# Hybrid decoder layer with a product-key expert feed-forward: gate value products on ScalarE, gate copies beside their own step, six weight buffers instead of three, new paces for the gathered rows

## The chip, the cores and the metric

The kernel runs on one core of one Trainium2 chip. The metric is the device time of one execution in microseconds (us); the time given is the median of three runs. Five engines work side by side, each on its own queue in order: PE (TensorE), DVE (VectorE), ACT (ScalarE), POOL (GpSimd) and SP (SyncE, which here issues the weight loads).

## The reference, cut to what matters

One layer: three gated token mixers on 256 tokens of width 1024, then a product-key expert layer, which takes two thirds of the time and is where the change lies. For every token and each of 8 heads, 16 of 16384 experts are chosen with softmax weights g, and then

```
a = gelu(einsum('btd,bthkd->bthk', hi, u_tab[expert]))
w = g * a
return einsum('bthk,bthkd->btd', w, v_tab[expert])
```

The tables `u_tab` and `v_tab` hold 16384 rows of 1024 float32 each, 64 MB per table.

## The kernel before, in words

The 256 tokens are split. For 160 of them (ND) the kernel computes all experts densely: the whole u table is streamed, 128 jobs of 128 experts (`u_job`, L1098), each 8 float32 products with 160 tokens into one of two PSUM tiles `pj`; Gelu on ACT moves the result into one slot of `RA` (jobs 0 to 63) or `RC` (64 to 127). Then the v table is streamed in 128 jobs (`v_job`, L1122), which sum over the slots. Between the two, the slots must be multiplied by the gate, a matrix that is zero except where a token chose an expert. The gate is built in 40 gate steps of 4 tokens: DVE makes one-hot rows `oo` (L1136) and multiplies two of them by the gate values, kept as two float16 parts, into `gi` (L1138); PE makes the gate of the 4 tokens in a PSUM tile `pg` with 8 small products (`g_mm`, L1143); `g_apply` (L1154) puts it down: ACT copies it to slots that no job has filled yet (L1163), which the later job then multiplies (L1108, L1111, L1112), and DVE multiplies it into filled slots (L1166).

For the other 96 tokens (NS) the chosen rows are gathered by index: 96 gathers of 128 rows from the u table, each followed by a dot product on DVE (L1044), then 96 from the v table, each followed by a weighted sum on DVE (L1049). One such row step (`x_step`, L1039) takes a row tile out of a ring of 6 (half a megabyte each), and then has POOL issue the gather for the tile six steps on (`x_load`, L1029, the indirect DMA of L1036).

The order of all queues is written by the program. After u job i, `run_todo` (L880) adds a pace to a purse and issues row steps at a cost of 1.2 each: pace 0.35 before the gates are open, 1.0 after, 1.45 in the v stage (`X_PACE`, L41). The selection of the experts is finished during the u stage; then `open_gates` (L1216) frees its memory and gate steps start, spread over the remaining jobs by `rate` (L1248). Both weight streams use one pool of three 1 MB tiles (`RAW_BUFS`, L42, pool `rawp`, L55), one for two jobs; `load_raw` (L65) issues the load on SP's queue, `ahead_split` (L259) says how far ahead (L271).

Of the kernel before, what the change touches and what calls it, by code (L numbers as in the profile page):

```python
# [10 lines left out]
F32 = mybir.dt.float32  # L11
F32R = mybir.dt.float32r
BF = mybir.dt.bfloat16
F16 = mybir.dt.float16
I32 = mybir.dt.int32
U32 = mybir.dt.uint32
AF = mybir.ActivationFunctionType
OP = mybir.AluOpType
# [12 lines left out]
GT = 4  # L31
N_G = ND // GT
# [5 lines left out]
N_X = 2 * NS  # L38
N_WARM = 12
SEL_PACE = 1.85  # L40
X_PACE = (0.35, 1.0, 1.45)  # L41
RAW_BUFS = 3  # L42
S_BUFS = 3
X_BUFS = 2 * S_BUFS
# [3 lines left out]
def hybrid_block(ctx, tc, xt, memt, wst, cmpw, subk, cols, cpe, fng, ut, vt, un, out):  # L48
    nc = tc.nc
# [5 lines left out]
    rawp = ctx.enter_context(tc.tile_pool(name="rawp", bufs=RAW_BUFS))  # L55
# [2 lines left out]
    psj = ctx.enter_context(tc.tile_pool(name="psj", bufs=2, space=PSUM))  # L58
    ctx.enter_context(tc.manual_schedule())

    raws = {}

    nc.scalar.preload_act_table_set("natural_log_exp_and_others")

    def load_raw(r):  # L65
        kind, i = raw_list[r]
        t = rawp.tile([128, 2, 1024], F32, name="raw")
        src = {"w": wst, "u": ut, "v": vt}[kind]
        nc.sync.dma_start(t, src[2 * i:2 * i + 2].rearrange("n p c -> p n c"))
        raws[r] = t  # L70


    raw_list = [("w", i) for i in range(N_W // 2)]
    job_raw = {}
# [16 lines left out]
    next_raw = [0]  # L91

    def prefetch(n):
        while next_raw[0] < min(n, len(raw_list)):
            load_raw(next_raw[0])
            next_raw[0] += 1
# [140 lines left out]
    order = [("w", i) for i in range(N_W)] + list(u_order)  # L237
# [16 lines left out]
    def ahead(key):  # L254
        run_deferred(pre=True)
        ahead_split(key)
        run_deferred()

    def ahead_split(key):  # L259
        n = pos[key] + LOOK  # L260
        while done_split[0] <= min(n, len(order) - 1):
            k = order[done_split[0]]
            r = job_raw[k[0], k[1] // 2]
            prefetch(r + 1)
            if k[0] == "w":
                split(k, 2 if k == ("w", 1) else 1)
            done_split[0] += 1
            nxt = done_split[0]
            if nxt < len(order):
                prefetch(job_raw[order[nxt][0], order[nxt][1] // 2] + 1)  # L270
        prefetch(min(len(raw_list), job_raw[order[min(n, len(order) - 1)][0], order[min(n, len(order) - 1)][1] // 2] + RAW_BUFS - 1))  # L271

    hA1 = big.tile([128, 8, T], F32R, name="hA1")
    hA2 = big.tile([128, 8, T], F32R, name="hA2")
# [488 lines left out]
    for j in range(8):  # L763
# [4 lines left out]
        a = s1[key].rearrange("p (k c) -> p k c", k=8)  # L768
# [41 lines left out]
    for ks in (range(0, 6), range(6, 8)):  # L810
        for i in range(2):
            a = s1["w", 58 + i].rearrange("p (k c) -> p k c", k=8)
# [37 lines left out]
    ring = ctx.enter_context(tc.tile_pool(name="ring", bufs=1))  # L850
# [3 lines left out]
    RA = ring.tile([128, 64, ND], F32, name="RA")  # L854
# [4 lines left out]
    sel = se.enter_context(tc.tile_pool(name="sel", bufs=1, side="right"))  # L859
# [20 lines left out]
    def run_todo(names, purse, budget):  # L880
        debt[purse] += budget
        while True:
            n = next((n for n in names if todo[n]), None)
            if n is None:
                debt[purse] = 0.0
                return
            if todo[n][0][0] > debt[purse]:
                return
            c, f = todo[n].pop(0)
            debt[purse] -= c  # L890
            f()

    def tick2(budget):
        run_todo((1, 0), "s", budget)
# [13 lines left out]

    io16 = sel.tile([128, 16], F16, name="io16")
    nc.gpsimd.iota(io16, pattern=[[1, 16]], base=0, channel_multiplier=0, allow_small_or_imprecise_dtypes=True)  # L910
    gt = ring.tile([128, N_G, 4, GT], F16, name="gt")
    sd, sel_done = {}, []

    def sel_open(t):
# [65 lines left out]
    def sel_e(t):  # L980
        p = psg.tile([128, 3, 128], F32, name="pg")
        for n, src in enumerate((sd["r", t, 0], sd["r", t, 1], sd["bv", t])):
            nc.tensor.transpose(p[:, n], src.rearrange("p h k -> p (h k)"), ident)
        nq_ = min(32, N_G - t * 32)
        g = gt[:, t * 32:t * 32 + nq_].rearrange("p q n e -> p n q e")
        pe = p[:, :, 0:nq_ * GT].rearrange("p n (q e) -> p n q e", e=GT)
        nc.scalar.activation(g[:, 0:3], pe, AF.Copy)
        nc.vector.tensor_tensor(g[:, 3], pe[:, 2], g[:, 2], op=OP.subtract)
        sel_done.append(t)


# [2 lines left out]
    xa = ring.tile([128, NS], F32, name="xa")  # L994
    xw = ring.tile([128, NS], F32, name="xw")
    xcol = [sum(m for _, m, _ in X_GROUPS[:g]) for g in range(len(X_GROUPS))]
    xrow, x_free, x_next = {}, [0], [0]

    def x_move(dst, src, g, c, n):
# [29 lines left out]
    def x_load(n):  # L1029
        if n >= N_X:  # L1030
            return
        g, c = X_ORDER[n % NS]
        c += xcol[g]
        t = (sp1, sp2)[n % 2].tile([128, D], F32, name=("s1", "s2")[n % 2])
        src = un if n < NS else vt.rearrange("a b c -> (a b) c")
        nc.gpsimd.indirect_dma_start(t, None, src, bass.IndirectOffsetOnAxis(ap=xi[:, c:c + 1], axis=0))  # L1036
        xrow[n] = t

    def x_step(n):  # L1039
        t = xrow.pop(n)  # L1040
# [50 lines left out]
    slots = {}  # L1091
# [22 lines left out]
    gs = {}  # L1114
# [7 lines left out]
    def v_job(i):  # L1122
        ahead(("v", i))
        for c in range(8):
            v_mm(i, c)
# [4 lines left out]
    def g_prep(q):  # L1130
        if q >= N_G:
            return
        oo = gp.tile([128, 4, 128, 2], F16, name="oo", tag="g2", bufs=4)
        gi = gp.tile([128, 2, 2, 128, 2], F16, name="gi", tag="g2", bufs=4)
        tk = gt[:, q].rearrange("p n (a e) -> p (n a) e", e=2)
        nc.vector.tensor_tensor(oo, io2[:, None].to_broadcast([128, 4, 128, 2]),  # L1136
                                tk[:, 0:4, None, :].to_broadcast([128, 4, 128, 2]), op=OP.is_equal)
        nc.vector.tensor_tensor(gi, oo[:, None, 0:2].to_broadcast([128, 2, 2, 128, 2]),  # L1138
                                tk[:, 4:8].rearrange("p (s a) e -> p s a e", s=2)[:, :, :, None, :]
                                .to_broadcast([128, 2, 2, 128, 2]), op=OP.mult)  # L1140
        gs[q] = (oo, gi)

    def g_mm(q):  # L1143
        if q >= N_G:
            return
        oo, gi = gs.pop(q)
        p = psg.tile([128, GT, 128], F32, name="pg")
        for k in range(GT):
            for s in range(2):
                nc.tensor.matmul(p[:, k], oo[:, 2 + k // 2, :, k % 2], gi[:, s, k // 2, :, k % 2],  # L1150
                                 start=(s == 0), stop=(s == 1))
        gs["p", q] = p

    def g_apply(q, n):  # L1154

        if ("p", q) not in gs:
            return
        c = slice(q * GT, q * GT + GT)
        pv = gs.pop(("p", q)).rearrange("p t i -> p i t")
        for dst, i0 in ((RA, 0), (slots["RC"], 64)):  # L1160
            m = min(max(n - i0, 0), 64)
            if m < 64:
                nc.scalar.activation(dst[:, m:, c], pv[:, i0 + m:i0 + 64], AF.Copy, scale=1.0 / GSCALE)  # L1163
            if m:
                d = dst[:, 0:m, c]
                nc.vector.scalar_tensor_tensor(d, pv[:, i0:i0 + m], 1.0 / GSCALE, d, op0=OP.mult, op1=OP.mult)  # L1166
        g_done[0] = q + 1
# [48 lines left out]
    def open_gates():  # L1216
        nonlocal gp
        se.close()
        hb.close()
        gp = ctx.enter_context(tc.tile_pool(name="gp", bufs=2))  # L1220
        rc = ctx.enter_context(tc.tile_pool(name="rc", bufs=1))
        slots["RC"] = rc.tile([128, 64, ND], F32, name="RC")
        g_prep(0)

    gp, q, opened, rate, owed = None, 0, False, 0.0, 0.0
    for i in range(128):
        owed += rate
        step_g = owed >= 1.0
        if step_g:
            owed -= 1.0  # L1230
            g_prep(q + 1)
            g_apply(q - 1, i)
        u_job(i)
        if step_g:
            g_mm(q)
            q += 1
        if i == 0:
            scores(14)
            scores(15)
            select(1)  # L1240
            select(0)
            x_rows()
        if not opened:
            tick2(SEL_PACE if i < 90 else 1e9)
            opened = len(sel_done) == 2
            if opened:
                open_gates()
                rate = (N_G + 2) / (125.0 - i)  # L1248
        run_todo(("x",), "x", X_PACE[0] if not opened else X_PACE[1])
    fg = big.tile([128, D], F32, name="hA1")  # L1250
    nc.gpsimd.dma_start(fg, bass.AP(tensor=fng.tensor, offset=fng.offset, ap=[[0, 128], [1, D]]))
# [2 lines left out]
    for g, (o, m, r) in enumerate(X_GROUPS):  # L1254
        for s in range(r):
            nc.vector.tensor_tensor(fold[:, g, o:o + m], fold[:, g, o:o + m], ident[:, s * m:s * m + m], op=OP.add)
    for i in range(125):
        v_job(i)
        run_todo(("x",), "x", X_PACE[2] if i < 118 else 1e9)
    for i in range(125, 128):  # L1260
        ahead(("v", i))

# [127 lines left out]
```

## Time and profile before

| what | us |
|---|---|
| median of 3 runs (lowest, highest) | 976.77 (976.39, 977.38) |
| the profiled execution's own time | 975.81 |
| its span in the trace | 974.1 |
| busy: PE, DVE | 912.5 (94%), 659.3 (68%) |
| busy: POOL, ACT | 321.1 (33%), 240.8 (25%) |
| moved by DMA | 285.12 MB, mean 293 GB/s |

The profile is of one execution and 1.7 us shorter than that execution's time. In it the u jobs run from 308 to 629 us, the gate steps from 452 to 624 us, and the v jobs from 630 to 960 us. A float32 job of 8 products stands as 16 PE instructions. Busy PE is not PE at its peak, since matmuls overlap: the start of one group to the start of the next is what a job takes. A wait is put down to what ended last.

### The profile page before, as it was taken

The numbers are of one execution on the slowest core, as the hardware profiler recorded it, in microseconds if no ns is written. First come the engines' busy times: TensorE is split into PE (matmuls) and PEld (weight loads), VectorE is DVE, ScalarE is ACT, GpSimd is POOL, SyncE is SP. The second block draws the span as 40 slices with busy tenths as digits, with TensorE's granted clock in tenths as the row PEclk, the third lists the DMA queues.
The fourth block names the chain that finished last, engine by engine and source line by source line (L and its number), as shares of the span: only waits on it lengthen the run. The fifth ranks groups of instructions, "written<-read, shape, count | busy, mean of one in ns | idle before, by whom it ended". The sixth has DMA issues, their size and how long they took to land.

```text
span 974.1 us, 17019 instructions
## 1 busy us (share of the span) xinstructions
PE 912.5 (94%) x6807; PEld 868.2 (89%) x6807; DVE 659.3 (68%) x1410; ACT 240.8 (25%) x585; POOL 321.1 (33%) x346
## 2 busy tenths in 40 slices
PE   8999999998998999999999999998999989999894
PEld 6999999898998999999999989988888888888884
DVE  7757677657678788998888899844444444544442
ACT  4754688744433112112111111100000000000001
POOL 7702000036740143113343344343333333333301
PEclk8999999999999999999999999999999999999998
DMA  7734444335543698888999999999999999999971
GB/s 281 240 130 141 155 139 140 137 126 171 174 145 115 197 391 295 312 309 313 377 371 353 364 351 359 370 408 408 408 410 408 408 409 408 409 409 408 408 306 43
DMA packets 76318, 285.12 MB, mean 293 GB/s; under 512 B 6880, under 2 KB 6928, under 8 KB 75856
## 3 DMA queue, kind: packets, MB, share of 16 engines
q1 hardware_dynamic: 47152, 181.15, 50.7%
q0 software_dynamic: 28800, 102.61, 26.9%
q8 instruction: 53, 0.87, 0.4%
q10 hardware_dynamic: 288, 0.29, 0.1%
q14 instruction: 25, 0.20, 0.1%
HBM read 282.63 MB, written 1.05 MB: 291 GB/s over the span
## 4 chain that ended last, share of the span: by engine, by line
PE 46%; DMA 24%; DVE 22%; ACT 3%; POOL 2%; issue 2%; POOLq 0%; SPq 0%; ACTq 0%
DMA raw<-in_vt_dram 23%; PE po L1119 11%; PE pj L1104 8%; PE pj L232 6%; DVE s L1044 6%; PE pj L233 6%; PE pj L234 6%; DVE gi L1138 2%; DVE oo L1136 2%; DVE RA L1166 1%; ACT RC L1163 1%; POOL t L782 1%; DMA raw<-in_ut_dram 1%; DVE RC L1112 1%; PE z L233 1%
## 5 line engine op out<-in xcount | busy, mean ns | idle before, releaser
L1104 PE MATMUL pj<-hA,raw 128*128 128x160 f32 x2048 | 291.2, 301 | 7.8 <-ACT ga L1111 5.8
L1104 PEld LDWEIGHTS pj<-hA,raw 128*128 128x128 f32 x2048 | 279.9, 190 | 11.2 <-ACT ga L1111 8.0
L1049 DVE SCALAR_TENSOR_TENSOR acc<-s,xw,acc 128x1024 f32<-128x1024 f32 x94 | 120.8, 1285 | 126.7 <-DMA s<-in_vt_dram,xi 126.7
L1036 POOL DMA_INDIRECT s<-in_un_dram,xi x96 | 113.0, 1177 | 210.8 <-DVE xa L1044 120.0
L1119 PE MATMUL po<-RC,raw 128*128 128x160 f32 x1024 | 148.8, 302 | 14.1 <-DMA raw<-in_vt_dram 13.3
L1119 PE MATMUL po<-RA,raw 128*128 128x160 f32 x1024 | 147.6, 302 | 15.0 <-DMA raw<-in_vt_dram 15.0
L1119 PEld LDWEIGHTS po<-RA,raw 128*128 128x128 f32 x1024 | 139.9, 190 | 22.7 <-DMA raw<-in_vt_dram 21.7
L1119 PEld LDWEIGHTS po<-RC,raw 128*128 128x128 f32 x1024 | 140.2, 190 | 22.4 <-DMA raw<-in_vt_dram 20.3
L1036 POOL DMA_INDIRECT s<-in_vt_dram,xi x96 | 90.4, 942 | 161.6 <-DVE acc L1049 147.5
L1044 DVE CUSTOM_DVE_ANT_0 s<-s,hA 128x1024 f32<-128x1024 f32 x96 | 116.8, 1219 | 37.6 <-DMA s<-in_un_dram,xi 37.5
L202 DVE TENSOR_TENSOR s<-raw,s 128x1024 fp32r<-128x1024 f32 (+1 forms) x77 | 100.7, 1312 | 28.7 <-ACT s L201 28.4
L201 ACT ACTIVATE s<-raw 128x1024 fp32r<-128x1024 f32 (+1 forms) x84 | 86.5, 1035 | 68.8 <-PE pj L233 45.0
L232 PE MATMUL pj<-hA,s 128*128 128x256 f32 x336 | 99.0, 295 | 0.1
L234 PE MATMUL pj<-hA,s 128*128 128x256 f32 x336 | 95.0, 283 | 0.0
L233 PE MATMUL pj<-hA,s 128*128 128x256 f32 x336 | 95.0, 283 | 0.0
L232 PEld LDWEIGHTS pj<-hA,s 128*128 128x128 f32 x336 | 64.3, 191 | 3.3 <-issue 1.8
L1181 ACT ACTIVATE RA<-pg 128x512 f32<-128x512 f32 x2 | 1.2, 592 | 263.1 <-PE pg L1272 263.1
L233 PEld LDWEIGHTS pj<-hA,s 128*128 128x128 f32 x336 | 64.3, 191 | 0.6 <-issue 0.5
L234 PEld LDWEIGHTS pj<-hA,s 128*128 128x128 f32 x336 | 64.2, 191 | 0.0
L1108 ACT ACTIVATE RA<-pj 128x160 f32<-128x160 f32 x64 | 19.3, 304 | 120.8 <-PE pj L1104 120.8
L1163 ACT ACTIVATE RC<-pg 128x256 f32<-128x256 f32 (+39 forms) x40 | 11.4, 284 | 123.1 <-DVE RA L1166 123.1
L780 POOL TENSOR_TENSOR t<-t,t 128x256 f32<-128x256 f32 x7 | 5.1, 734 | 106.0 <-DVE t L779 106.0
(340 smaller groups left out, 1257.9 us busy)
## 6 DMA issues: line engine op xcount, KB each, us to landing
raw<-in_ut_dram SPq DMA_DIRECT2D x64, 1024.0 KB, 7.6
raw<-in_vt_dram SPq DMA_DIRECT2D x64, 1024.0 KB, 10.5
raw<-in_wst_dram SPq DMA_DIRECT2D x39, 1024.0 KB, 5.0
raw<-in_wst_dram SPq DMA_DIRECT2D x4, 512.0 KB, 7.5
s<-in_un_dram,xi POOLq DMA_INDIRECT x96, 8.2
s<-in_vt_dram,xi POOLq DMA_INDIRECT x96, 14.2
x<-in_memt_dram SPq DMA_DIRECT2D x1, 1024.0 KB, 7.1
cw<-in_cmpw_dram POOLq DMA_DIRECT2D x1, 1024.0 KB, 7.3
```

Source lines behind the costliest of these rows:

```text
L201: nc.scalar.activation(a[:, c], src[:, c], AF.Copy)
L202: eng.tensor_tensor(b[:, c], src[:, c], a[:, c].bitcast(F32), op=OP.subtract)
L232: nc.tensor.matmul(dst, l1, r1, start=first, stop=False)
L233: nc.tensor.matmul(dst, l1, r2, start=False, stop=False)
L234: nc.tensor.matmul(dst, l2, r1, start=False, stop=last)
L1036: nc.gpsimd.indirect_dma_start(t, None, src, bass.IndirectOffsetOnAxis(ap=xi[:, c:c + 1], axis=0))
L1044: nc.vector.tensor_tensor_reduce(t, t, hnat[:, g], 1.0, 0.0, OP.mult, OP.add, xa[:, c:c + 1])
L1049: nc.vector.scalar_tensor_tensor(acc[:, g], t, xw[:, c:c + 1], acc[:, g], op0=OP.mult, op1=OP.add)
L1104: nc.tensor.matmul(p, a[:, k], hT[:, k, 0:ND], start=(k == 0), stop=(k == 7))
L1119: nc.tensor.matmul(po[c // 2][:, c % 2], a[:, c * 128:c * 128 + 128], slot(i), start=(i == 0 and c % 2 == 0), stop=(i == 127), skip_group_ ...
L1136: nc.vector.tensor_tensor(oo, io2[:, None].to_broadcast([128, 4, 128, 2]), tk[:, 0:4, None, :].to_broadcast([128, 4, 128, 2]), op=OP.is_equal)
L1163: nc.scalar.activation(dst[:, m:, c], pv[:, i0 + m:i0 + 64], AF.Copy, scale=1.0 / GSCALE)
```

## The change

The gate values are kept in float32 (`gv`: the value, and what float16 loses of it). The product of one-hot rows and gate values moves from one DVE instruction (1024 elements) to eight ACT instructions of 128 elements each with a scale per partition (`g_gi`). `g_apply` is cut in two: the copies on ACT (`g_copy`) are issued right after the gate product of their own step, the DVE products at the start of the next job. From `open_gates` on a second pool of three weight tiles takes turns with the first, and loads are issued up to five tiles ahead instead of two. Row steps have pace 1.3 instead of 1.0 in the gate stage, and in the v stage the steps that are left are spread evenly over 116 jobs.

```diff
-X_PACE = (0.35, 1.0, 1.45)
+X_PACE = (0.35, 1.3)
...
-    raws = {}
+    raws, more = {}, {"from": None, "depth": RAW_BUFS - 1}
...
-        t = rawp.tile([128, 2, 1024], F32, name="raw")
+        pool = rawp if more["from"] is None or (r - more["from"]) // RAW_BUFS % 2 else more["pool"]
+        t = pool.tile([128, 2, 1024], F32, name="raw")
...
-        prefetch(min(len(raw_list), job_raw[...] + RAW_BUFS - 1))
+        prefetch(min(len(raw_list), job_raw[...] + more["depth"]))
...
-    gt = ring.tile([128, N_G, 4, GT], F16, name="gt")
+    gt = ring.tile([128, N_G, 2, GT], F16, name="gt")
+    gv = ring.tile([128, N_G, 2, GT], F32, name="gv")
...
-        nc.scalar.activation(g[:, 0:3], pe, AF.Copy)
-        nc.vector.tensor_tensor(g[:, 3], pe[:, 2], g[:, 2], op=OP.subtract)
+        hi = sel.tile([128, 32, GT], F16, name="hi")[:, 0:nq_]
+        nc.scalar.activation(g, pe[:, 0:2], AF.Copy)
+        nc.scalar.activation(v[:, :, 0], pe[:, 2], AF.Copy)
+        nc.scalar.activation(hi, pe[:, 2], AF.Copy)
+        nc.vector.tensor_tensor(v[:, :, 1], pe[:, 2], hi, op=OP.subtract)
...
-        nc.vector.tensor_tensor(gi, oo[:, None, 0:2].to_broadcast([128, 2, 2, 128, 2]),
-                                tk[:, 4:8].rearrange("p (s a) e -> p s a e", s=2)[:, :, :, None, :]
-                                .to_broadcast([128, 2, 2, 128, 2]), op=OP.mult)
-        gs[q] = (oo, gi)
+        gs["o", q] = oo
+
+    def g_gi(q):
+        if q >= N_G:
+            return
+        oo = gs.pop(("o", q))
+        gi = gp.tile([128, 2, 2, 128, 2], F16, name="gi", tag="g2", bufs=4)
+        for s in range(2):
+            for k in range(GT):
+                nc.scalar.activation(gi[:, s, k // 2, :, k % 2], oo[:, k // 2, :, k % 2], AF.Copy,
+                                     scale=gv[:, q, s, k:k + 1])
+        gs[q] = (oo, gi)
...
+        more["pool"] = ctx.enter_context(tc.tile_pool(name="raw2", bufs=RAW_BUFS))
+        more["from"], more["depth"] = next_raw[0], 2 * RAW_BUFS - 1
...
     for i in range(128):
+        if late is not None:
+            g_apply(late, i)
+            late = None
         owed += rate
-        step_g = owed >= 1.0
+        step_g = owed >= 1.0 and q < N_G
         if step_g:
             owed -= 1.0
             g_prep(q + 1)
-            g_apply(q - 1, i)
         u_job(i)
         if step_g:
             g_mm(q)
+            g_copy(q, i + 1)
+            g_gi(q + 1)
+            late = q
             q += 1
...
-                rate = (N_G + 2) / (125.0 - i)
+                g_gi(0)
+                rate = N_G / (124.0 - i)
...
+    x_done = [k for k in range(N_X) if k not in xrow and k < x_seen[0]]
+    pace = 1.2 * (N_X - len(x_done)) / 116.0
     for i in range(125):
         v_job(i)
-        run_todo(("x",), "x", X_PACE[2] if i < 118 else 1e9)
+        run_todo(("x",), "x", pace if i < 118 else 1e9)
```

## Rows read from the trace of the kernel before

**Rows 1.** The page's part 4: the chain that ended last.

```profile
PE 46%; DMA 24%; DVE 22%; ACT 3%; POOL 2%; issue 2%; POOLq 0%; SPq 0%; ACTq 0%
DMA raw<-in_vt_dram 23%; PE po L1119 11%; PE pj L1104 8%; PE pj L232 6%; DVE s L1044 6%; PE pj L233 6%; PE pj L234 6%; DVE gi L1138 2%; DVE oo L1136 2%; DVE RA L1166 1%; ACT RC L1163 1%; POOL t L782 1%; DMA raw<-in_ut_dram 1%; DVE RC L1112 1%; PE z L233 1%
```

**Rows 2.** Windows: stretch and length, busy by engine (instructions), PEclk, DMA share, GB/s.

```profile
380.00:450.00 70.00, 70.00 (x518) 70.00 (x517) 66.20 (x220) 11.51 (x35) 13.05 (x14) 1.00 0.86 305
450.00:630.00 180.00, 173.12 (x1419) 168.14 (x1417) 156.23 (x344) 32.69 (x173) 71.02 (x57) 1.00 0.97 360
630.00:940.00 310.00, 282.02 (x1957) 267.32 (x1958) 151.60 (x152) 0.24 (x1) 110.95 (x117) 1.00 1.02 408
```

**Rows 3.** DMA in the gate stage, 450 to 630 us: rate by fortieths, sum, gathers to landing.

```profile
GB/s 297 337 350 395 350 399 386 340 358 347 380 391 411 365 329 328 368 341 381 381 361 340 359 364 346 401 349 330 322 369 383 381 370 310 342 376 376 354 333 392
DMA packets 17190, 64.75 MB, mean 360 GB/s; under 512 B 1421, under 2 KB 1421, under 8 KB 17174
...
s<-in_un_dram,xi POOLq DMA_INDIRECT x57, 7.9
```

**Rows 4.** DMA in the v stage, 630 to 940 us: sum, queues, gathers to landing.

```profile
DMA packets 33735, 126.61 MB, mean 408 GB/s; under 512 B 2880, under 2 KB 2880, under 8 KB 33714
...
q1 hardware_dynamic: 16634, 64.12, 51.7%
q0 software_dynamic: 17080, 62.18, 50.4%
...
s<-in_vt_dram,xi POOLq DMA_INDIRECT x96, 14.2
```

**Rows 5.** Timeline of PE in the v stage: start, length, line [idle before].

```profile
634.84 4.61 PE L1119 MATMUL po<-RA,raw 128*128 128x160 f32 x32 [0.29 <-DMA raw<-in_vt_dram]
639.80 4.61 PE L1119 MATMUL po<-RA,raw 128*128 128x160 f32 x32 [0.34 <-DMA raw<-in_vt_dram]
...
939.35 6.79 PE L1119 MATMUL po<-RC,raw 128*128 128x160 f32 x48 [0.34 <-DMA raw<-in_vt_dram]
945.97 1.88 PE L1267 MATMUL pg<-acc,fold 128*128 128x512 f32 x4
```

**Rows 6.** Timeline in the gate stage: a gate step and two jobs on PE.

```profile
539.79 0.62 PE L1150 MATMUL pg<-gi,oo 128*128 128x128 f16 x8
540.25 4.56 PE L1104 MATMUL pj<-hA,raw 128*128 128x160 f32 x32
...
544.65 0.62 PE L1150 MATMUL pg<-gi,oo 128*128 128x128 f16 x8
```

**Rows 7.** Timeline in the gate stage: DVE, one row step and one gate step.

```profile
546.92 1.22 DVE L1044 CUSTOM_DVE_ANT_0 s<-s,hA 128x1024 f32<-128x1024 f32 x1
548.06 0.08 DVE L1044 DVE_READ_ACCUMULATOR2_ANT xa<- 128x1 f32 x1
548.06 0.69 DVE L1136 TENSOR_TENSOR oo<-io,gt 128x1024 f16<-128x1024 f16 x1
548.79 0.69 DVE L1138 TENSOR_TENSOR gi<-oo,gt 128x1024 f16<-128x1024 f16 x1
549.40 0.42 DVE L1166 SCALAR_TENSOR_TENSOR RA<-pg,RA 128x256 f32<-128x256 f32 x1
550.22 0.29 DVE L1166 SCALAR_TENSOR_TENSOR RC<-pg,RC 128x128 f32<-128x128 f32 x1 [0.40 <-ACT RC L1163]
```

**Rows 8.** Timeline of ACT: two in a row in the gate stage; two at the end.

```profile
549.91 0.28 ACT L1163 ACTIVATE RC<-pg 128x128 f32<-128x128 f32 x1 [3.18 <-DVE RA L1166]
550.08 0.23 ACT L1108 ACTIVATE RC<-pj 128x72 f32<-128x72 f32 x1
550.19 0.25 ACT L1111 ACTIVATE ga<-pj 128x88 f32<-128x88 f32 x1
...
961.11 0.60 ACT L1181 ACTIVATE RA<-pj 128x512 f32<-128x512 f32 x1 [3.68 <-PE pj L1272]
...
964.96 0.72 ACT L1198 ACTIVATE RA<-RA,fs 128x512 f32<-128x512 f32 x1 [2.59 <-POOL fs L1193]
```

**Rows 9.** Line L1036 (POOL's gathers), 450 to 630 us: count, ns min/median/max.

```profile
L1036 POOL DMA_INDIRECT s<-in_un_dram,xi x57: 932/1146/1897, 452.2 to 629.1; - x57
```

**Rows 10.** The page's part 5: weighted sums of rows in the v stage.

```profile
L1049 DVE SCALAR_TENSOR_TENSOR acc<-s,xw,acc 128x1024 f32<-128x1024 f32 x94 | 120.8, 1285 | 126.7 <-DMA s<-in_vt_dram,xi 126.7
```

More of the change, by code (lines that the diff above doesn't have):

```diff
@@ L270, in ahead_split @@
                 prefetch(job_raw[order[nxt][0], order[nxt][1] // 2] + 1)
-        prefetch(min(len(raw_list), job_raw[order[min(n, len(order) - 1)][0], order[min(n, len(order) - 1)][1] // 2] + RAW_BUFS - 1))
+        prefetch(min(len(raw_list), job_raw[order[min(n, len(order) - 1)][0], order[min(n, len(order) - 1)][1] // 2] + more["depth"]))
     hA1 = big.tile([128, 8, T], F32R, name="hA1")
@@ L985, in sel_e @@
         g = gt[:, t * 32:t * 32 + nq_].rearrange("p q n e -> p n q e")
+        v = gv[:, t * 32:t * 32 + nq_]
         pe = p[:, :, 0:nq_ * GT].rearrange("p n (q e) -> p n q e", e=GT)
-        nc.scalar.activation(g[:, 0:3], pe, AF.Copy)
-        nc.vector.tensor_tensor(g[:, 3], pe[:, 2], g[:, 2], op=OP.subtract)
+        hi = sel.tile([128, 32, GT], F16, name="hi")[:, 0:nq_]
[3 more added lines that the diff above has]
+        nc.vector.tensor_tensor(v[:, :, 1], pe[:, 2], hi, op=OP.subtract)
         sel_done.append(t)
@@ L996, in hybrid_block @@
     xcol = [sum(m for _, m, _ in X_GROUPS[:g]) for g in range(len(X_GROUPS))]
+    x_seen = [0]
     xrow, x_free, x_next = {}, [0], [0]
@@ L1037, in x_load @@
         xrow[n] = t
+        x_seen[0] = n + 1
     def x_step(n):
@@ L1133, in g_prep @@
         oo = gp.tile([128, 4, 128, 2], F16, name="oo", tag="g2", bufs=4)
-        gi = gp.tile([128, 2, 2, 128, 2], F16, name="gi", tag="g2", bufs=4)
         tk = gt[:, q].rearrange("p n (a e) -> p (n a) e", e=2)
         nc.vector.tensor_tensor(oo, io2[:, None].to_broadcast([128, 4, 128, 2]),
-                                tk[:, 0:4, None, :].to_broadcast([128, 4, 128, 2]), op=OP.is_equal)
-        nc.vector.tensor_tensor(gi, oo[:, None, 0:2].to_broadcast([128, 2, 2, 128, 2]),
-                                tk[:, 4:8].rearrange("p (s a) e -> p s a e", s=2)[:, :, :, None, :]
-                                .to_broadcast([128, 2, 2, 128, 2]), op=OP.mult)
+                                tk[:, :, None, :].to_broadcast([128, 4, 128, 2]), op=OP.is_equal)
+        gs["o", q] = oo
[8 more added lines that the diff above has]
+                                     scale=gv[:, q, s, k:k + 1])
         gs[q] = (oo, gi)
@@ L1152, in g_mm, with g_copy @@
         gs["p", q] = p
-    def g_apply(q, n):
-        if ("p", q) not in gs:
-            return
+    def g_copy(q, n):
+        pv = gs["p", q].rearrange("p t i -> p i t")
         c = slice(q * GT, q * GT + GT)
-        pv = gs.pop(("p", q)).rearrange("p t i -> p i t")
         for dst, i0 in ((RA, 0), (slots["RC"], 64)):
@@ L1163, in g_apply @@
                 nc.scalar.activation(dst[:, m:, c], pv[:, i0 + m:i0 + 64], AF.Copy, scale=1.0 / GSCALE)
+    def g_apply(q, n):
+        pv = gs.pop(("p", q)).rearrange("p t i -> p i t")
+        c = slice(q * GT, q * GT + GT)
+        for dst, i0 in ((RA, 0), (slots["RC"], 64)):
+            m = min(max(n - i0, 0), 64)
             if m:
@@ L1222, in open_gates @@
         slots["RC"] = rc.tile([128, 64, ND], F32, name="RC")
+        more["pool"] = ctx.enter_context(tc.tile_pool(name="raw2", bufs=RAW_BUFS))
+        more["from"], more["depth"] = next_raw[0], 2 * RAW_BUFS - 1
         g_prep(0)
-    gp, q, opened, rate, owed = None, 0, False, 0.0, 0.0
+    gp, q, opened, rate, owed, late = None, 0, False, 0.0, 0.0, None
     for i in range(128):
+        if late is not None:
+            g_apply(late, i)
+            late = None
         owed += rate
-        step_g = owed >= 1.0
+        step_g = owed >= 1.0 and q < N_G
         if step_g:
```

## The prediction

> **What bounds the kernel now.** I read the chain that ended last first. Its largest line that is not PE is the wait for v tiles, 23% of the span; DVE lines of the gate stage come after it [rows 1]. Then the windows, to see what is full where: before the gates the DMA engines move 305 GB/s, in the gate stage (450 to 630 us) 360, in the v stage (630 to 940 us) 408, and there every fortieth is alike while the gate stage swings between 297 and 411 [rows 2 to 4]. So the v stage runs at a ceiling of about 408 GB/s, and the gate stage now and then touches it and lies 12% below on the mean. PE shows the price: in the v stage 32 instructions (two jobs) come every 4.96 us, with a wait for a v tile before each; where no wait comes between, three jobs take 6.62 us, 2.21 each [rows 5]. 125 jobs would be 276 us and take 310 to 316.
>
> Who shares the v stage? Weights took 64.1 MB and gathers 62.2 [rows 4]. DVE waits for a gather before all but a few of its 94 sums [rows 10], and has nothing else to do; the gathers go as fast as DMA lets them, whatever pace the program gives them. Each gather moved out of the v stage frees 0.52 MB of a full resource.
>
> In the gate stage PE needs 2.20 us per job and 0.46 per gate step [rows 6]. The 57 gathers there [rows 9], at 1.0/1.2 = 0.83 per job, are 68 jobs. The floor of PE is 68 x 2.20 + 40 x 0.46 = 168 us; the stage takes 179. DVE is nearly full (156 of 180 us busy, [rows 2]) and stands on the chain with `gi`, `oo` and the row steps.
>
> The effective limit over both stages is therefore bytes: 64.75 + 126.61 = 191.4 MB from 450 to 940 us [rows 3, 4]. At 408 GB/s all along this is 469 us and not 490. **21 us is the most that the change can get from DMA**, for it takes no byte away. PE's floor for the two stages, 168 + 276 = 444 us, is lower and doesn't bind.
>
> **The change, part by part.**
> *Pace 1.3.* 1.3/1.2 = 1.08 row steps per job, in 68 jobs 73.7 and not 57: 16.7 gathers, 8.75 MB, move to the gate stage. On DVE each is 1.14 us (start to start, [rows 7]), 19 us in all. On POOL each is an issue of 1.15 us [rows 9], 19 us more on 71 busy of 180 [rows 2], beside other work; POOL has nothing else queued there.
>
> *Second pool, depth 5.* Three more 1 MB tiles are fetched as soon as the gates open, 3.1 MB that would else load in the v stage. On SP's queue only the order in time changes; a load still waits for the job that frees its tile, now for a tile three pairs older. In the v stage more loads queue, but the ceiling stands, so this moves bytes and adds none. It also takes the beat out of the wait: a late tile no longer stops PE at once.
>
> *Value products on ACT.* DVE loses 40 `gi` at 0.61 us start to start, 24 us [rows 7]. ACT gains 320 instructions. None like it is in the trace of the gate stage. Bounds: 512 elements with a scale per partition take 0.72 us, and elements cost (0.60 - 0.23)/440 = 0.84 ns each [rows 8], so 128 take 0.72 - 0.32 = 0.40 us, if nothing overlaps. From below: 72 elements take 0.23 us, the next starts after 0.11, so 128 without such a scale start 0.16 apart [rows 8]. I take 0.40 less the overlap of 0.12, 0.28 (the row with the scale is the nearest in kind): 8 x 0.28 = 2.3 us per gate step, 92 us in all, between 51 and 128. ACT is busy 33 of 180 us [rows 2], so it has the room.
>
> But order matters: `gi` of the next step stands on ACT behind the copy, which waits for the gate product. From the start of the product: 0.62 to its end, 0.2 copy, 2.3 + 0.1 for `gi`: 3.2 us. PE is back for the next gate product after 0.46 + 2.20 = 2.66 us if the next job is a gate step too, after 4.86 if not. The rate is 40 steps in 64 jobs, 1.6 jobs apart, so 16 of 39 intervals are one job long: 16 x 0.6 = 9 us of waits (none at the low end, 16 x 1.5 = 24 at the high end). Behind the eight instructions the next job's Gelu waits; two `pj` tiles give it a whole job of slack.
>
> *Copies with their own step.* DVE's second product waits 0.40 us for ACT's copy [rows 7], 40 times 16 us at most. The copy now comes a job earlier, and this wait goes. DVE over the stage: 19 - 24 - 16 = 21 us less, so DVE stops being the limit. What is late next are the gathers.
>
> *Selection copies.* Two more ACT copies of under 0.4 us at each of two places, some 1 us, beside PE. *Even v pace.* Nothing: DVE and POOL hold only row steps there, and the order of program text beside v jobs binds no engine. If that cover failed, row steps would wait for v jobs' DVE work, of which there is none before the end.
>
> **The sum.** Bytes of the gate stage become 64.75 + 8.75 + 3.1 = 76.6 MB, and PE's floor with ACT's waits is 168 + 9 = 177 us, so it asks for 433 GB/s: DMA becomes its bound too. At the full 408 it takes 188 us, and all 21 us are won. But a ring of 6 gathers ahead of an in-order DVE is not a perfect feed, and the stage has swung by over 100 GB/s. I take 396, three quarters of the way from 360 to 408: 76.6/0.396 = 193.4 us. The v stage then has 191.4 - 76.6 = 114.8 MB, 281.4 us, just above PE's 276. Sum 474.8 and not 490: 15 us won. The last jobs and the finish after 940 us are unchanged. The profiled execution's 975.8 us becomes 960.6; it is 1.0 below the median of the runs, so **961.5 us**. The gate stage itself gets longer, by some 13 us, and the v stage shorter by some 28.
>
> HBM Reference of the Trainium skill (Specifications) states about 425 GB/s for a core that streams alone; by it the ceiling would give 191.4/0.425 = 450 us, 40 won. No window here goes past 411 for long, so the trace disagrees and 408 stands.
>
> **The rivals.**
> *DVE in order, starved.* Gathers land after 7.9 us in the gate stage and 14.2 in the full v stage [rows 3, 4]. With 6 tiles a step may come every (14.2 + 1.15 + 1.14)/6 = 2.7 us, and pace 1.08 at 2.5 us per job wants one every 2.3. A row step that waits holds `oo`, the products and, through them, PE; weights then pile up and DMA idles. If the gate stage stays near 375 GB/s: 76.6/0.375 + 281.4 = 485.7, 4 us won, **972**. Against it: weights stop asking once six tiles are full, which shortens landing.
>
> *Gate stage already full (the other side).* Its DMA share is 0.97 at 360 GB/s [rows 2]. If that is its true ceiling, 11.85 MB move from a stage that does 408 to one that does 360: 11.85 x (1/0.360 - 1/0.408) = 3.9 us lost, **981**. It decides wherever the stage cannot pass 362. Against it: share is no fullness, for it is 0.86 at 305 and 1.02 at 408, less per byte at the higher load [rows 2], and fortieths of 399 and 411 stand in the stage [rows 3]. HBM Reference (Specifications) also gives about 358 GB/s as a core's effective part; by it the gate stage would be at its end. The v stage's 408 disagrees.
>
> *ACT becomes the bound (slower).* If one product took over 0.5 us the loop 0.62 + 0.2 + 8 x 0.5 = 4.8 us would fill every interval. At 0.6 each it is 5.6: 16 x 2.9 + 23 x 0.75 = 64 us of waits, and the gate stage 232 us; then v on 276 to 282, near 510, some 20 slower, **997**. Against it: the 0.40 bound above. ScalarE: Activation LUTs of the skill (Rules for kernel authors) wants products on VectorE, up to three times faster; this trace's DVE does 1024 in 0.69 us, so the rule holds per element but not for a full DVE beside an idle ACT.
>
> *It does nothing:* the row steps moved are given back by loads that come later, within 2 us of before.
>
> **How the numbers follow.** Forecast (8 us or more won) 0.66; DVE starved (3 to 8 won) 0.18; nothing 0.06; gate stage full 0.06; ACT bound 0.04. Faster by over 0.2% (2 us, about what a measurement of this kernel can tell from no change): 0.84; same 0.07; slower 0.09. The low end is 21 us won, 956, less 1 for a shorter tail: 955. The high end takes in the starved case: 972.
>
> **What would show it.** Gate stage at 390 to 408 GB/s and some 190 us long; 73 or 74 row steps in it; ACT's products 0.40 us each with starts 0.28 apart, 100 to 130 us of ACT busy there; PE waiting for ACT's `gi` under 1 us before about 16 gate products; no wait of DVE on L1163's copy; the v stage still at 408, near 282 us. Wrong would be: a gate stage below 375 GB/s with DVE waiting for gathers, a v stage away from 408, or products above 0.5 us.

## The result and the profile after

The changed kernel took **964.12 us** (median of 4, 963.58 to 967.50), the kernel before in the same set 977.08. The ratio is 0.9875, with a 95% interval of 0.9851 to 0.9898: 13 us faster by the medians, where 15 were forecast. The profiled execution took 964.13 us with a span of 962.4 against 974.1, 11.7 less.

First the windows of the changed kernel, with the columns of [rows 2].

```profile
450.00:630.00 180.00, 173.21 (x1362) 164.53 (x1361) 139.64 (x324) 126.46 (x487) 72.44 (x69) 0.99 1.02 406
639.00:916.00 277.00, 262.69 (x1865) 253.94 (x1864) 134.95 (x123) 0.39 (x2) 94.83 (x101) 1.00 1.03 409
...
920.00:930.00 10.00, 10.00 (x76) 10.00 (x75) 0.00 (x0) 0.00 (x0) 0.00 (x0) 1.00 0.44 176
930.00:940.00 10.00, 9.58 (x54) 7.43 (x53) 0.32 (x1) 0.00 (x0) 0.00 (x0) 1.00 0.00 0
```

The gate stage now moves 406 GB/s and not 360, the v stage stays at its ceiling, and DMA falls idle near 924.3 us (176 GB/s in ten us are 4.3 us at 408). Before the change it did so near 943.8 us, reckoned in the same way:

```profile
940.00:950.00 10.00, 10.00 (x59) 8.09 (x58) 2.57 (x2) 0.00 (x0) 0.00 (x0) 1.00 0.41 155
```

Next the timeline of PE in the v stage, which answers to [rows 5], and the last row step on DVE.

```profile
638.64 95.79 PE L1127 MATMUL po<-RA,raw 128*128 128x160 f32 x704
734.60 4.61 PE L1127 MATMUL po<-RA,raw 128*128 128x160 f32 x32 [0.17 <-DMA raw<-in_vt_dram]
...
905.23 4.61 PE L1127 MATMUL po<-RC,raw 128*128 128x160 f32 x32 [0.32 <-DMA raw<-in_vt_dram]
910.20 24.29 PE L1127 MATMUL po<-RC,raw 128*128 128x160 f32 x176 [0.36 <-DMA raw<-in_vt_dram]
934.33 1.88 PE L1296 MATMUL pg<-acc,fold 128*128 128x512 f32 x4
...
914.78 1.28 DVE L1057 SCALAR_TENSOR_TENSOR acc<-s,xw,acc 128x1024 f32<-128x1024 f32 x1 [1.23 <-DMA s<-in_vt_dram,xi]
```

The v stage starts 9 us later (638.6, not 630.0) and ends 11.6 earlier (934.3, not 946.0). It has three parts: 44 jobs without a wait, which use up the lead of six full tiles (PE takes a tile, two jobs, in 4.4 us, and DMA brings one in 4.96); then a wait per pair, a pair every 4.96 us, as before; and from 910 on 11 jobs without a wait. The last gather's sum starts at 914.8. Until then the gathers take half of DMA; when they end, the weights have all of it, DMA is through at 924, and PE has yet to work off what lies in the tiles. Before, 3 jobs came after the last wait.

In the gate stage, from the page, from POOL's gathers and from the waits (450 to 639 us; in all, times, longest):

```profile
L1154 ACT ACTIVATE gi<-oo,gv 128x128 f16<-128x128 f16 x320 | 99.3, 426 | 14.8 <-DVE oo L1143 14.3
```

```profile
L1043 POOL DMA_INDIRECT s<-in_un_dram,xi x73: 934/939/1681, 453.6 to 638.8; - x73
```

```profile
DVE s L1052 <- DMA s<-in_un_dram,xi: 11.9, 17, 1.5
...
PE pg L1165 <- ACT gi L1154: 5.3, 9, 0.9
```

73 gathers were issued, as forecast; DVE waited 17 times for one, and PE 9 times for ACT's `gi`, under 1 us each.

### The profile page after: what moved, and what is told of

Read it like the earlier page. It is cut to its first block, busy times and chain, and to the rows that moved or that the text cites. A ratio compares the mean times of both kernels' runs of the same rounds, so it can differ in the third digit from the quotient of the medians.

```text
span 962.4 us, 17333 instructions
## 1 busy us (share of the span) xinstructions
PE 913.5 (95%) x6807; PEld 871.6 (91%) x6807; DVE 629.5 (65%) x1371; ACT 337.5 (35%) x912; POOL 309.4 (32%) x346
## 4 chain that ended last, share of the span: by engine, by line
PE 48%; DMA 19%; issue 14%; POOL 9%; DVE 8%; ACT 2%; POOLq 0%; SPq 0%; DVEq 0%; ACTq 0%
DMA raw<-in_vt_dram 16%; PE po L1127 16%; POOL s L1043 7%; PE pj L233 6%; PE pj L234 6%; PE pj L235 6%; PE pj L1112 6%; DMA s<-in_un_dram,xi 1%; DMA raw<-in_ut_dram 1%; POOL t L783 1%; DVE s L203 1%; DVE s L1052 1%; DVE ti L902 1%; DVE sc L903 1%; PE z L234 1%
## 5 line engine op out<-in xcount | busy, mean ns | idle before, releaser
L1043 POOL DMA_INDIRECT s<-in_un_dram,xi x96 | 101.2, 1054 | 185.4 <-DVE xa L1052 142.3
L1127 PE MATMUL po<-RA,raw 128*128 128x160 f32 x1024 | 141.9, 300 | 3.4 <-DMA raw<-in_vt_dram 3.4
L1154 ACT ACTIVATE gi<-oo,gv 128x128 f16<-128x128 f16 x320 | 99.3, 426 | 14.8 <-DVE oo L1143 14.3
```

The costliest lines, as they stand in the source:

```text
L1127: nc.tensor.matmul(po[c // 2][:, c % 2], a[:, c * 128:c * 128 + 128], slot(i), start=(i == 0 and c % 2 == 0), stop=(i == 127), skip_group_ ...
L1154: nc.scalar.activation(gi[:, s, k // 2, :, k % 2], oo[:, k // 2, :, k % 2], AF.Copy, scale=gv[:, q, s, k:k + 1])
```

## The experiments

Each kernel was timed in a set with the kernel before; ratios are to that, with the 95% interval. "Jobs left" are the v jobs that PE did after its last wait for a tile, ahead of the last three, in the one profiled execution of each kernel (that of e6 took 4.4 us more than its median, those of e11 and e12 some 3 more). "Pace" is that of the gate stage. Early copies are issued right after the gate product of their own step, late ones beside DVE's products of the same step.

| kernel | pace | tiles | gi on | copies | us | ratio (interval) | jobs left |
|---|---|---|---|---|---|---|---|
| before | 1.0 | 3 | DVE | late | 977.1 | 1 | 3 |
| changed | 1.3 | 6 | ACT | early | 964.1 | 0.9875 (0.9851, 0.9898) | 11 |
| e1, old v pace | 1.3 | 6 | ACT | early | 965.5 | 0.9862 (0.9836, 0.9888) | 11 |
| e2 | 1.3 | 3 | ACT | early | 972.5 | 0.9955 (0.9935, 0.9975) | 17 |
| e3 | 1.0 | 6 | ACT | early | 969.7 | 0.9905 (0.9882, 0.9927) | 1 |
| e4 | 1.15 | 6 | ACT | early | 958.5 | 0.9799 (0.9775, 0.9824) | 3 |
| e5 | 1.3 | 6 | DVE | early | 963.1 | 0.9852 (0.9831, 0.9873) | 9 |
| e6 | 1.15 | 6 | DVE | early | 960.3 | 0.9813 (0.9794, 0.9832) | 5 |
| e7 | 1.3 | 3 | DVE | late | 986.8 | 1.0085 (1.0066, 1.0104) | 17 |
| e8 | 1.3 | 6 | ACT | late | 975.5 | 0.9975 (0.9959, 0.9992) | 11 |
| e9 | 1.3 | 6 | DVE | late | 972.9 | 0.9944 (0.9923, 0.9964) | 9 |
| e10 | 1.0 | 3 | DVE | early | 969.2 | 0.9905 (0.9882, 0.9928) | 3 |
| e11 | 1.3 | 3 | DVE | early | 971.7 | 0.9938 (0.9914, 0.9963) | 17 |
| e12 | 1.15 | 3 | ACT | early | 971.6 | 0.9922 (0.9899, 0.9945) | 11 |

**e1, the pace of the v stage.** The edit:

```diff
-    pace = 1.2 * (N_X - len(x_done)) / 116.0
+    pace = 1.45
```

> The changed kernel with the v stage's row steps at the old pace 1.45. Theory of bytes and queues: DVE and POOL hold nothing but row steps in the v stage, so gathers go as fast as DMA serves their queue, whatever the program's pace: 964 us within 1.5, last weighted sum near 915 us in the trace as before this edit. Rival (the even pace slows the gathers and leaves room for weights): gathers end 25 us or more earlier, PE waits more for v tiles until then, 966 to 972 us.

Measured 965.5 us, last sum at 916.6: no difference beyond the interval. The v stage's pace does nothing that can be told, as forecast: its queues on DVE and POOL hold row steps alone.

**e2, three tiles.** The two lines that make and announce the second pool were taken out.

> The changed kernel without the second pool: three weight tiles and loads two ahead throughout. Theory of bytes: the moved gathers still fill the gate stage (64.75 + 8.75 = 73.5 MB, at 400 GB/s 184 us) and the v stage stays at 408, where weights cannot run ahead: PE ends 6 us after the last waited tile, not 16, so 960 to 967 us, near the changed kernel. Rival (the depth of the weight buffer hides the landings and is what made the kernel faster): the v stage is back at a wait of a tile per pair with the beat of before and the gate stage waits for u tiles: 970 to 978 us.

Measured 972.5, in the rival's range. Of its account one half holds: the v stage has a wait for a tile per pair from its start, but in the gate stage PE waits only 0.9 us in all for u tiles. The last sum is at 906.8 us, 8 earlier than in the changed kernel, and then:

```profile
900.00:910.00 10.00, 9.60 (x71) 9.36 (x70) 4.01 (x4) 0.00 (x0) 0.00 (x0) 1.00 0.79 295
910.00:920.00 10.00, 10.00 (x76) 10.00 (x75) 0.00 (x0) 0.00 (x0) 0.00 (x0) 1.00 0.72 233
920.00:930.00 10.00, 10.00 (x76) 10.00 (x75) 0.00 (x0) 0.00 (x0) 0.00 (x0) 1.00 0.78 265
930.00:940.00 10.00, 10.00 (x76) 10.00 (x75) 0.00 (x0) 0.00 (x0) 0.00 (x0) 1.00 0.68 239
```

```profile
904.30 37.22 PE L1127 MATMUL po<-RC,raw 128*128 128x160 f32 x272 [0.40 <-DMA raw<-in_vt_dram]
```

For 37 us PE works without a wait, and DMA, with three tiles to fill, goes at PE's pace, some 240 GB/s. My theory had the ceiling right and had left out that the gathers finish first. Three more tiles are a lead of three pairs, six jobs: 17 jobs are left here and 11 with six tiles.

**e3 and e4, the pace of the gate stage.** `X_PACE = (0.35, 1.0)` and `(0.35, 1.15)`.

> The changed kernel with pace 1.0 in the gate stage as before the change: 57 row steps there and not 74. Theory of bytes: the gate stage asks for 64.75 + 3.1 = 67.9 MB in 177 to 180 us, some 380 GB/s, so DMA is left unused by 7% of the stage; the v stage has 123.5 MB, 302 us; PE ends its 125 v jobs near 938 to 942 us: 968 to 972 us. Rival (relief of DVE by ACT's products and earlier copies is the gain): gate stage shorter by 10 us than in the changed kernel and the whole at 958 to 964 us.

> The changed kernel with pace 1.15 in the gate stage: 65 row steps there. Theory of bytes with equal shares of the queues: 72 MB still fill the gate stage's 178 to 182 us, and in the v stage gathers and weights end together near 925 us, so PE is left with two or three jobs and not 11 when DMA falls idle: 957 to 962 us, faster than the changed kernel. Rival (more gathers in the gate stage is always better): between pace 1.0 and 1.3, 965 to 969 us.

969.7 and 958.5 us: both in the range of the theory of bytes. Less in the gate stage is better than the change's 1.3, and too little is worse. But e3 came to its time by another way than the theory's, which had PE at v jobs until 938 us or later. Its jobs end at 928.9, and the gathers come last: PE is done with its weights and waits for sums.

```profile
928.85 1.57 PE L1296 MATMUL pg<-acc,fold 128*128 128x512 f32 x2
938.49 2.08 PE L1296 MATMUL pg<-acc,fold 128*128 128x512 f32 x2 [8.07 <-DVE acc L1057]
```

In e4 both streams end together, the last sum at 924.9 us, three jobs after the last wait:

```profile
923.80 6.79 PE L1127 MATMUL po<-RC,raw 128*128 128x160 f32 x48 [0.27 <-DMA raw<-in_vt_dram]
930.43 1.88 PE L1296 MATMUL pg<-acc,fold 128*128 128x512 f32 x4
```

**e5 and e6, products back on DVE.** `g_prep` makes `gi` with the one DVE instruction of before, `g_gi` does nothing, and the selection keeps the gate values as before; e6 with pace 1.15.

> The changed kernel with the value products back on DVE (one instruction of 1024, as before), all else as changed: pace 1.3, six tiles, copies early. Theory of bytes: at pace 1.3 DVE needs 84 (row steps) + 26 + 24 + 26 + 14 = 174 us of about 189 and has some 12 to 30 us of waits in its order, so the gate stage grows by 5 to 15 us and falls below 400 GB/s: 966 to 972 us. Rival (ACT's products bring nothing, DMA is the limit either way): 962 to 966 us. Rival (the eight instructions on ACT hold PE and cost more than they give): under 962 us.

> The same at pace 1.15: nine row steps fewer in the gate stage, 10 us less of DVE, some 165 us of 180. Theory of bytes: DVE just fits beside DMA's 177 us, the stage ends within 5 us of the kernel with pace 1.15 and products on ACT: 958 to 963 us. Rival (DVE's relief is needed at any pace): 965 us or more.

963.1 and 960.3 us, where ACT's products gave 964.1 and 958.5: the intervals overlap in both pairs. For e5 the rival was right that the products on ACT bring nothing. In e5 PE waited 12.7 us for DVE's `gi` (5.3 for ACT's in the changed kernel) and DVE was fuller, but DMA was still at its ceiling:

```profile
500.00:550.00 50.00, 46.13 (x382) 44.97 (x380) 43.56 (x99) 10.54 (x50) 18.97 (x19) 1.00 1.03 408
550.00:600.00 50.00, 44.59 (x361) 44.08 (x362) 46.42 (x101) 8.58 (x44) 19.18 (x19) 0.97 1.03 408
```

**e7, the pace alone.** On the kernel before, `X_PACE = (0.35, 1.3, 1.45)`.

> The kernel before with one number changed: pace 1.3 in the gate stage. No part of the relief of DVE and no second pool. Theory of bytes: DVE needs 174 us and 16 more of waiting for ACT's copies, so it stretches the gate stage to 195 to 205 us at 360 to 378 GB/s, and with three tiles PE ends the v stage alone: 970 to 976 us, little won. Rival (pace alone fills the gate stage): 964 to 969 us.

986.8 us, **slower than before** and outside both forecasts. The waits of its gate stage:

```profile
ACT RC L1163 <- DVE RA L1166: 143.6, 39, 5.4
...
PE pj L1104 <- ACT ga L1111: 12.1, 15, 2.0
```

The same two in the kernel before:

```profile
ACT RC L1163 <- DVE RA L1166: 123.1, 40, 4.3
...
PE pj L1104 <- ACT ga L1111: 5.8, 9, 0.9
```

One of the windows of e7's gate stage:

```profile
500.00:550.00 50.00, 46.06 (x367) 44.48 (x366) 44.69 (x100) 8.64 (x49) 24.62 (x19) 0.97 0.99 369
```

ACT, with nothing much to do, stands 144 us before its copy, until DVE has taken its product from the same tile, `pg`. ACT is in order, so Gelu, which empties `pj`, stands behind that copy, and PE waits for `pj`. More row steps make DVE later, and this chain carries its lateness to PE, whose waits for Gelu double. The v stage starts at 644.5 us, and with three tiles the end is e2's, 17 jobs in 37.2 us without a wait.

**e8, copies late, products on ACT.** `g_copy` is called right ahead of `g_apply`, at the start of the next job.

> The changed kernel with ACT's gate copies issued at the start of the next job, beside DVE's gate products, as before the change. Theory of bytes: DVE waits again for the copy, up to 40 x 0.4 = 16 us spread over the stage, but DMA sets its length: 963 to 967 us. Rival (the early copy is a part of the gain): 968 to 974 us.

975.5 us: the rival's side, and above its 974. The waits show more than it said:

```profile
DVE RA L1185 <- ACT RC L1176: 53.7, 39, 4.1
ACT gi L1154 <- DVE oo L1143: 49.6, 34, 2.8
```

Placed there, the copy stands on ACT behind the eight products, which wait for DVE's `oo`, and DVE waits for the copy: two in-order queues that hold each other. So e8 is no clean measure of the copies; e9 to e11 are.

**e9, e10, e11, copies late and early with products on DVE.** e9 is before with pace 1.3 and the second pool; e10 is before with `g_copy` and `g_apply` split and placed as in the change, which also issues DVE's products at the next job and not at the next gate step, and spreads 40 steps where 42 were spread; e11 is e10 at pace 1.3.

> The kernel before with pace 1.3 and the second pool, but with value products on DVE and copies and products of a gate step issued together one step late, as before. Theory of the chained queues: ACT's copy waits for DVE's product of the same gate tile, Gelu stands behind it, so every lateness of DVE stops PE; the stage stays near 372 GB/s and the pool gives its 8 us: 976 to 981 us. Rival (fuller weight buffers are enough): 963 to 968 us.

> The kernel before with one part of the change: ACT's copies with their own gate step and DVE's products at the start of the next job; pace 1.0, three tiles, value products on DVE. Theory of the chained queues: the gate stage falls from 179 us to 170 to 176, PE's floor being 168, and no more, since at pace 1.0 DVE was only a little late; the v stage is bound by bytes as before: 969 to 974 us. Rival (the copies matter only beside ACT's products): 976 to 979 us.

> The same with pace 1.3: the kernel with three tiles and pace 1.3, but value products on DVE. Theory of the chained queues: the place of the products is indifferent, so 969 to 975 us, the time of that kernel (972.5), and 12 to 17 us under the kernel with pace 1.3 alone (986.8). Rival (pace 1.3 needs the products off DVE): 979 to 987 us.

972.9, 969.2 and 971.7 us. Late against early copies: e7 to e11 with three tiles 15 us, e9 to e5 with six 10 us, before to e10 at pace 1.0 8 us. These are prices of the split as a whole: no run moves the copies and leaves all else. That the chain is what it cuts is argued from the waits. In e10 ACT's wait for DVE is gone, and the long wait of its queue is for PE; PE waits 0.5 us for Gelu and not 5.8, and the v stage starts at 622.7 us, 7.3 earlier than before:

```profile
ACT RC L1108 <- PE pj L1104: 117.1, 61, 2.5
DVE RC L1112 <- ACT ga L1111: 15.2, 27, 1.4
```

```profile
622.65 8.93 PE L1119 MATMUL po<-RA,raw 128*128 128x160 f32 x64
```

In e11 PE's wait for `ga` is gone from the list, 12.1 us in e7, and the v stage starts at 632.9 us, 11.6 earlier than e7's. e10 and e11 came as the theory of the chained queues said. e9 fell between the forecasts, since the pool gave 14 us and not 8. Its chain is e7's, and its v stage starts at 644.1 us, but DMA moves more in the gate stage than e7's 365 to 377 GB/s, as it can with three more tiles to fill while PE stands:

```profile
ACT RC L1164 <- DVE RA L1167: 134.4, 37, 5.4
...
PE pj L1105 <- ACT ga L1112: 13.5, 16, 2.0
```

```profile
450.00:630.00 180.00, 162.18 (x1315) 155.12 (x1314) 161.18 (x347) 29.79 (x161) 86.67 (x66) 1.00 1.00 390
```

**e12, three tiles at pace 1.15.**

> The changed kernel with three tiles and pace 1.15. Theory of bytes and equal queue shares: gathers and weights end nearly together, PE is left with some 4 jobs and not 17, so the second pool is worth 3 to 5 us at this pace and not 8: 961 to 965 us. Rival (three tiles cost the v stage the same at any pace): 966 to 970 us.

971.6 us, the rival's side and slower than it said: the pool is worth 13 us here. I had expected 4 jobs left and the trace has 11. The gate stage reaches 389 GB/s where e4, with six tiles, had 404; first e12, then e4:

```profile
450.00:630.00 180.00, 178.49 (x1444) 172.56 (x1443) 139.50 (x325) 128.75 (x500) 67.82 (x65) 1.00 1.00 389
...
920.00:930.00 10.00, 9.78 (x72) 9.79 (x73) 2.20 (x2) 0.00 (x0) 0.00 (x0) 1.00 0.67 257
930.00:940.00 10.00, 10.00 (x75) 10.00 (x75) 0.00 (x0) 0.00 (x0) 0.00 (x0) 1.00 0.71 224
```

```profile
450.00:630.00 180.00, 179.20 (x1452) 173.58 (x1451) 138.90 (x330) 127.40 (x499) 67.86 (x66) 1.00 1.02 404
```

15 GB/s over 180 us are 2.7 MB, near the 3.1 MB of three tiles and worth 6.6 us at 408 (an estimate). The rest is lost at the end, where DMA goes at PE's pace again.

The table shows one thing more: pool and pace pay only together. At pace 1.0 the pool brings nothing (e10 969.2, e3 969.7, which differ also in where `gi` is made), and with three tiles the pace brings nothing (e10, e12, e11: 969.2, 971.6, 971.7).

## Why the prediction was right or wrong

*Bytes as the limit: right, but the match in time is in part luck.* DMA was to be done with its 191.4 MB after 474.8 us, at 924.8; it was near 924.3. But that sum ends at 940 us in the kernel before, when DMA still had 1.55 MB to move (155 GB/s in ten us), which it left to the unchanged finish. On one footing DMA came to its end 19.5 us earlier, from 943.8 to 924.3, and not 15.2: near the 21 that were given as the most. The gate stage was to run at 396 GB/s for 193 us; it ran at 406 for 189, better fed than I took it to be.

*"The last jobs and the finish after 940 us are unchanged": wrong, and the term that cost the difference.* PE was to end 6.6 us after the last wait, as before; it ended 24.1 after, with 11 jobs and not 3. Counted from DMA's end, its jobs ended 2.2 us later before (946.0) and 10.0 later now (934.3). These 7.8 us bring the 19.5 down to the 11.7 by which the spans differ. The forecast had 4.3 us too little from DMA and did not see the 7.8 at the end; that the two errors work against each other, and leave it so near, is luck. Gathers and weights share DMA almost evenly while both ask, with three tiles and with six (shares below), and with 17 gathers fewer in the v stage the gathers were done first. The bound on the gain was given as bytes alone, when the order in which two streams end mattered too. e4 is the test: fewer gathers moved, both streams end together, 5.6 us faster than the change.

*"DVE stops being the limit" by the products: wrong part credited.* The sum counted 24 us of `gi` and 16 of waiting for the copy off DVE. e5, e6 and e11 show that the 24 bring nothing in time. What paid was the other half, and for a reason that I did not see: not DVE's 0.40 us before its second product, but ACT's 3.18 us before the copy, which stand in the first line of [rows 8]. Idle time of an idle engine looked free; a Gelu stood behind it.

*Value products.* 8 take 2.48 us in the trace, 0.42 each with starts 0.29 apart; 0.40 and 0.28 were forecast. PE was to wait for them 16 times, 0.6 us each; it did 9 times, 5.3 us in all. ACT was busy 126 of 180 us, as said.

*Second pool: "moves bytes and adds none": wrong.* In the sum its 3.1 MB only pass from one stage near the ceiling to the other, so it was put at nothing. It was worth 8.4 us at pace 1.3 (e2), 13 at 1.15 (e12 to e4) and nothing at 1.0 (e10 to e3). Without it DMA falls below its ceiling at the end, since three tiles let it go only at PE's pace, some 240 GB/s.

*Even v pace: nothing. Right* (e1).

*The rivals.* DVE starved: DVE did wait 17 times for gathers, 11.9 us, and the stage stayed at the ceiling. Gate stage full at 360: 406 settles it. HBM Reference of the Trainium skill (Specifications) gives about 358 GB/s as a core's effective part, and says that a core that streams alone measures well above it. This trace, of one core alone at 406 to 409, agrees with the latter. ACT as the bound: not at 0.42 us. The mechanism that can make this change slower was not among my rivals; it is e7's chain, which is gone where the copies come early.

## What to carry to other kernels

Where an engine waits long but has little to do, look at what stands behind the waiting instruction in its queue before calling the idle time free; splitting a step so that a queue no longer waited for a busier engine was worth 8 to 15 us here, moving 24 us of work off that busier engine nothing. When two streams share a full resource, balance them so that they end together: with six tiles pace 1.15 beats both 1.0 and 1.3, and the best kernel run is e4, 958.5 us, 19 under before in its set. A part tried by itself can lose what it wins in company: the pace alone cost 9 us, and with early copies but three tiles it won nothing.

## What the runs showed of the hardware

Shares of the two DMA queues in the v stage (640 to 900 us) of e12, with three weight tiles, and of the changed kernel, with six; the columns are packets, MB and share of 16 engines.

```profile
q1 hardware_dynamic: 13921, 53.68, 51.6%
q0 software_dynamic: 14393, 52.41, 50.6%
```

```profile
q1 hardware_dynamic: 14118, 54.42, 52.3%
q0 software_dynamic: 14152, 51.55, 49.9%
```

With twice as many tiles to load into, the weights' part of the bytes of the two queues goes from 50.6 to 51.4%. DMA: Bandwidth & Descriptors of the Trainium skill (Queues, rings and completion order) says that a DMA engine takes turns between the queues that have work for it. These near halves agree.

In e3 the granted clock falls twice to half of full speed, the lower level, 1.2 GHz, as PE runs out of work. The first fall follows PE's wait of 1.87 us for its last v tile, until 925.4 us; the second comes during its wait of 8 us for the sums:

```profile
925.00:930.00 5.00, 4.56 (x18) 3.75 (x18) 2.57 (x2) 0.00 (x0) 1.61 (x3) 0.66 0.97 365
930.00:935.00 5.00, 0.42 (x1) 0.00 (x0) 4.34 (x4) 0.00 (x0) 0.67 (x1) 0.84 0.68 251
935.00:940.00 5.00, 1.51 (x2) 0.84 (x3) 3.36 (x3) 0.00 (x0) 0.00 (x0) 0.50 0.02 7
940.00:945.00 5.00, 4.67 (x11) 2.08 (x9) 0.29 (x1) 0.00 (x0) 0.00 (x0) 0.64 0.00 0
```

```profile
925.44 3.61 PE L1127 MATMUL po<-RC,raw 128*128 128x160 f32 x16 [1.87 <-DMA raw<-in_vt_dram]
...
940.36 3.50 PE L1296 MATMUL pj<-acc,fold 128*128 128x512 f32 x4
```

It is back at 1.00 from 945 us on. The v job at 925.4 us took 3.4 us to the start of what follows it, where a job else takes 2.2, and the four products at 940.4 took 3.50 us, where four such took 1.88 in the changed kernel: a late stream costs a little more than its wait.
